# An ordered seven-product stage, a later S5 gate, and set-up work of block 0 placed anew

## The chip, the cores and the metric

One NeuronCore of one Trainium2 chip runs the kernel. The metric is the device time of one execution in microseconds (us); the median of three runs of the kernel before is 3021.39 us.

## The reference, cut to what matters

One layer over 2048 tokens of width 1024, in float32. The input is normalised, and one matrix gives twelve pieces of 512 columns and four merge gates of 1024 columns. Four branches read the pieces; each is gated by a SiLU path, projected to 1024 columns, weighted by a sigmoid gate and summed; an output matrix follows and `x` is added.

```python
h = rms_norm(x, norm_g)
proj = h @ w_in                      # 12 * 512 + 4 * 1024 columns
a_out = s5_branch(ssm_u, ...) * silu(ssm_gate)       # diagonal state space scan, then a GLU
b_out = retention_branch(ret_q, ret_k, ret_v) * silu(ret_gate)
c_out = diff_attn_branch(diff_q, diff_k, diff_v, ...) * silu(diff_gate)
m_out = memory_branch(mem_q, mem_n, ...) * silu(mem_gate)
br = einsum('bsnc,ncd->bsnd', stack(a_out, b_out, c_out, m_out), w_branch)
out = x + sum(sigmoid(merge + b_merge) * br, n) @ w_out
```

## The kernel before, in words

The tokens go in two blocks of 1024, one after the other through the same stages. Every float32 product is made of three matmuls on a high and a low part of each operand (`mm3`): ACT casts the high part (`hi`), DVE or POOL subtracts it from the value for the low part (`lo`).

**Stages of a block**, with their stretches in block 0 and block 1: retention (8 to 332 us and 1499 to 1730 us), differential attention with the S5 input at its end (to 682 and 2216 us), the seven-product stage (to 1140 and 2667 us), merge of the branches with memory attention and the S5 gate beside it (to 1399 and 2921 us), output (to 1499 and 3016 us).

**Retention** (L896 to L966) works in 32 units of four heads by eight token tiles. `Events` holds each step with a time in units: project, scale, turn (L913), score (L922), values (L930 to L940), finish, store. In block 0, events before unit 6 load, scale and turn the input tiles (`Norm`, L564 to L589), `setup_vectors` (L142) issues 15 small DMAs and one transpose, and `setup_s5` (L179) is advanced nine steps a unit from unit 6 on. For each of four groups of four S5 pairs it makes `gm` and turns it (L371), reads and turns `cm` (L388), makes `ca`, and multiplies `ca` by `bb` (L425).

**The seven-product stage** (`projections`, L1398) forms 2x2 block products with seven instead of eight multiplications. One column pair is first done plainly, four products of 24 matmuls of 128x512 (`proj_tr`). Meanwhile `x_mix` (L1368) makes the mixed inputs t2, t3, t4, t1 for four slices k. Then 21 column pairs run seven products each, 147 steps of 12 matmuls. `prepare(g + LEAD)` makes the weight of the product four steps ahead (ACT `p_h` L1304, POOL `p_l` L1305, DVE sums L1315 to L1329), `product` issues the matmuls (L1343), `collect` combines PSUM banks on DVE (L1352 to L1364) and stores. In 16 S5 scans, one for every seven steps, `s5_scan` (L998 to L1048) does two matmuls (L1002), a rotation, a scan (L1019) and another rotation on DVE, then four matmuls (L1033, L1034) that read `s_x` (L1027, L1028); `carry` is saved by L1029.

**Merge** (`Merge.run`) has 32 units of 24 matmuls: a branch product gets its gate in DVE (L1276), and POOL adds it to `merged` (L1277). Branch data come back from DRAM through four raw buffers `w_r` that weights share (`load`, L1221 to L1223). Beside the merge run the memory attention, then the S5 gate: `s5_z` reads z, `s5_zsplit` splits it (ACT L1064, DVE L1066), `s5_glu` multiplies and gates it (ACT L1088). **Output** splits `merged` (L1525, L1526), multiplies by `w_out`, and adds `x` (L1539).

**What sets the order.** Every engine takes its instructions in the order of its queue. A list scheduler of the framework fixes these orders when the kernel is built: the place in the program is a priority, and an instruction whose inputs the scheduler takes for ready may go ahead. Pools are given out again by address, so a tile waits for the last user of its space.

## Time and profile before

| what | us |
|---|---|
| median of three runs (3019.27 to 3024.44) | 3021.39 |
| the profiled execution | 3017.78 |
| its span, first to last instruction | 3016.0 |
| PE busy | 2872.6 |
| DVE busy | 1958.8 |
| ACT busy | 1336.7 |
| POOL busy | 1234.1 |

The profiled execution's time has 1.8 us around its span. PE is TensorE's matmul row, DVE VectorE, ACT ScalarE, POOL GpSimd, SP the queue that issues nearly all DMAs. PE's busy time also holds what a lower granted clock adds.

### The profile page before, as it was taken

To read this page: it belongs to the slowest core of one execution; us is meant where nothing else is said; L and a number is where in the kernel's file an instruction comes from. 1 tells how busy PE (TensorE), PEld (TensorE's weight loads), DVE (VectorE), ACT (ScalarE), POOL (GpSimd) and SP (SyncE) were. 2 spreads that over 40 slices of the span, in tenths; PEclk is the share of its full clock that TensorE was granted. 3 is DMA by queue.
4 is the path that set the end of the run, shared out by engine and by line. 5 is a ranking of instruction groups with operands and counts; after the bars stand their busy time and mean duration, and the time that the engine had idled before them with its cause. 6 is when DMAs were issued, how large, how long until landed. Compare 5 with 4: busy or idle time off the path is not lost. (4 is left out here: it accounts for less than half of the span.)

```text
span 3016.0 us, 43039 instructions
## 1 busy us (share of the span) xinstructions
PE 2872.6 (95%) x14258; PEld 2372.2 (79%) x14258; DVE 1958.8 (65%) x4622; ACT 1336.7 (44%) x3365; POOL 1234.1 (41%) x1157
## 2 busy tenths in 40 slices
PE   7888999998999999999999999999999999999999
PEld 6776777777888888777788878778878888887777
DVE  7785477766756645656543378888777666546654
ACT  4223355563343344423433357776743444444332
POOL 3443543324444443555132242332244444435660
PEclk9999999999999999999999999999999999999999
DMA  4433422223444336555521220220224444355552
GB/s 135 108 96 85 124 67 71 71 89 122 147 154 147 132 110 207 191 181 168 162 78 37 64 72 17 63 62 17 64 96 148 154 147 142 126 189 170 190 173 92
DMA packets 319645, 351.74 MB, mean 117 GB/s; under 512 B 26735, under 2 KB 238782, under 8 KB 319422
## 3 DMA queue, kind: packets, MB, share of 16 engines
q1 hardware_dynamic: 317118, 340.60, 35.9%
q0 software_dynamic: 2304, 8.39, 0.9%
q8 instruction: 112, 1.84, 0.3%
q14 instruction: 111, 0.91, 0.1%
HBM read 247.99 MB, written 100.93 MB: 116 GB/s over the span
## 5 line engine op out<-in xcount | busy, mean ns | idle before, releaser
L1305 POOL TENSOR_TENSOR p_l<-p_r,p_h 128x512 fp32r<-128x512 f32 x260 | 359.8, 1387 | 439.9 <-ACT p_h L1304 436.9
L74 PE MATMUL mm<-w5h,xh 128*128 128x512 f32 x1024 | 436.7, 426 | 5.5 <-ACT xh L588 2.7
L75 PE MATMUL mm<-w5l,xh 128*128 128x512 f32 x1024 | 406.8, 397 | 3.1 <-POOL w5l L454 3.0
L76 PE MATMUL mm<-w5h,xl 128*128 128x512 f32 x1024 | 408.9, 399 | 0.0
L138 POOL TENSOR_TENSOR rms_r<-rms_m,mhalf 128x1 f32<-128x1 f32 (+1 forms) x228 | 177.1, 778 | 498.9 <-DVE rms_m L136 428.4
L1304 ACT CAST p_h<-p_r 128x512 fp32r<-128x512 f32 x260 | 160.3, 621 | 365.7 <-DVE p_r L1318 109.4
L769 ACT ACTIVATE pr<-sc,nm 128x512 f32<-128x512 f32 (+3 forms) x320 | 200.4, 627 | 148.2 <-DVE nm L767 146.6
L76 PEld LDWEIGHTS mm<-w5h,xl 128*128 128x128 f32 x1024 | 194.8, 190 | 44.1 <-issue 0.4
L74 PEld LDWEIGHTS mm<-w5h,xh 128*128 128x128 f32 x1024 | 195.9, 191 | 36.1 <-ACT xh L588 3.1
L75 PEld LDWEIGHTS mm<-w5l,xh 128*128 128x128 f32 x1024 | 196.0, 191 | 31.8 <-POOL w5l L454 4.3
L75 PE MATMUL sc<-br_l,w1h 128*128 128x512 f32 x496 | 197.1, 397 | 7.6 <-DVE br_l L1223 7.6
L74 PE MATMUL sc<-br_h,w1h 128*128 128x512 f32 x496 | 200.3, 404 | 3.8 <-DVE mg_g L1276 3.6
L767 DVE TENSOR_REDUCE nm<-sc 128x1 f32<-128x512 f32 (+3 forms) x320 | 193.1, 604 | 9.0 <-PE sc L763 5.0
L76 PE MATMUL sc<-br_h,w1l 128*128 128x512 f32 x496 | 196.3, 396 | 0.0
L1277 POOL TENSOR_TENSOR mg<-mg,mg_g 128x512 f32<-128x512 f32 x96 | 142.0, 1483 | 88.4 <-DVE mg_g L1276 80.3
L817 PEld LDWEIGHTS o<-vt,at 128*128 128x128 f32 x1088 | 141.0, 191 | 38.3 <-ACT at L810 30.2
L817 PE MATMUL o<-vt,at 128*128 128x128 f32 x1088 | 150.9, 278 | 17.2 <-ACT at L810 17.1
L471 POOL TENSOR_TENSOR w1l<-w_r,w1h 128x512 fp32r<-128x512 f32 x86 | 119.4, 1402 | 114.2 <-ACT w1h L470 107.1
L454 POOL TENSOR_TENSOR w5l<-w_r,w5h 128x512 fp32r<-128x512 f32 x72 | 96.9, 1350 | 114.4 <-ACT w5h L453 79.6
L1343 PE MATMUL sc<-xl,p_h 128*128 128x512 f32 x336 | 131.3, 391 | 3.4 <-DVE xl L1378 3.4
L1343 PE MATMUL mm<-xh,p_h 128*128 128x512 f32 x336 | 133.7, 398 | 0.3 <-ACT p_t L1413 0.3
L1343 PE MATMUL sc<-xh,p_h 128*128 128x512 f32 x336 | 131.4, 391 | 1.0 <-ACT p_h L1304 0.5
(397 smaller groups left out, 7654.2 us busy)
## 6 DMA issues: line engine op xcount, KB each, us to landing
p_r<-in_w_in SPq DMA_DIRECT2D x88, 512.0 KB
w_r<-in_w_in SPq DMA_DIRECT2D x144, 256.0 KB
me_d<-p_t SPq DMA_DIRECT2D x128, 256.0 KB
mg_g<-me_d SPq DMA_DIRECT2D x64, 512.0 KB
s_m<-mats_d SPq DMA_DIRECT2D x32, 640.0 KB
w_r<-in_w_branch SPq DMA_DIRECT2D x64, 256.0 KB
w_r<-br SPq DMA_DIRECT2D x64, 256.0 KB
n_x<-in_x SPq DMA_DIRECT2D x16, 512.0 KB
```

The source lines that it names most:

```text
L74: PE.matmul(out, l[0], r[0], start=first, stop=False)
L75: PE.matmul(out, l[0], r[1], start=False, stop=False)
L76: PE.matmul(out, l[1], r[0], start=False, stop=last)
L138: G.tensor_tensor(r, m, mhalf[:, 0:n], op=ALU.pow)
L471: G.tensor_tensor(lo, raw, hi.bitcast(F32), op=ALU.subtract)
L767: V.tensor_reduce(nm, s[:, 0:n], axis=AX.X, op=ALU.max, negate=True)
L769: A.activation(e[:, 0:n], s[:, 0:n], AF.Exp, bias=nm, accum_out=self.zz[:, m, c:c + 1])
L817: PE.matmul(self.o[:, 0:128], self.at[c][:, q * 128:(q + 1) * 128], self.st["vts"][c][:, q, :], start=c == 0 and q == 0, stop=c * 4 + q == ...
L1277: G.tensor_tensor(dst, dst, t, op=ALU.add)
L1304: A.copy(hi, x)
L1305: G.tensor_tensor(lo, x, hi.bitcast(F32), op=ALU.subtract)
L1343: PE.matmul(o, l[:, k, :], r, start=first and k == 0 and q == 0, stop=k == 3 and q == 2, skip_group_check=True)
```

## The change

- **Ordered stage.** The whole of `projections` is put under `tc.manual_schedule` for DVE, ACT, POOL and PE: these engines keep the order of the program there. DMAs on SP are not ordered.
- **Its start.** `x_mix` yields after each cast and each subtraction and makes t1 before t4; its steps are written between the plain products, t4's behind the first three steps of the seven-product loop. The two low parts of the first column go from POOL to DVE. The S5 pool opens at step 5, and the first scan's loads move from step 1 to step 5.
- **Its end.** Branch 2's data are requested five to six steps ahead of their split; the first branch weight is read at step n - 10 and split at n - 5.
- **Set-up.** `cm` and `ca` are made ahead of `gm`'s transposes; one yield fewer a group.
- **Block 0.** Retention's values, finish and store come 0.4 units later. Input tiles have five buffers and are loaded a unit earlier; `setup_vectors` moves from 0.3 to 2.5.
- **Merge.** Branch data get four raw buffers of their own (`b_r`), gate tiles four buffers. From unit 16 on the second half's add is done by DVE. z is read at q = 7 of the loop, split from 10, multiplied from 26 (before: 0, 4, 20).
- **Output.** The residual is read two tiles ahead into three buffers; the sums have two.

```diff
+    ORDERED = {x.engine for x in (V, A, G, PE)}
...
             tt(gm[:, 1], tmp[0], tmp[1], ALU.add)
             yield
-            yield
+            cm = p.tile([16, 2, 2 * m, 64], F32, name="cm")
+            for i, nm in enumerate(("ssm_c_re", "ssm_c_im")):
+                DMA.dma_start(out=cm[:, i], in_=a[nm][0].rearrange("g h p -> h g p")[:, 2 * j0:2 * j0 + 2 * m, :])
...
+            ts(ca[:, 1], tmp[0], -1.0, ALU.mult)
             yield
             for j in range(0, m, 2):
                 pt = ps_tr()
...
-            cm = p.tile([16, 2, 2 * m, 64], F32, name="cm")
...
-            ts(ca[:, 1], tmp[0], -1.0, ALU.mult)
             yield
             yield
             for g2 in range(2):
...
-            self.x = self.p.tile([128, D], F32, name="n_x", bufs=(3, 2)[b])
+            self.x = self.p.tile([128, D], F32, name="n_x", bufs=(5, 2)[b])
...
-                events.at(i + 3.3, x.values)
-                events.at(i + 4.1, x.finish)
+                late = (0.4, 0.0)[b]
+                events.at(i + 3.3 + late, x.values)
+                events.at(i + 4.1 + late, x.finish)
                 if t % 4 == 3:
-                    events.at(i + 4.7, x.store)
+                    events.at(i + 4.7 + late, x.store)
...
             self.w0 = self.cx.enter_context(pool("w0", side="right"))
-            self.raw = self.raw_w(0)
...
+        def request(self, n, k):
+            raws = []
+            for hf in range(2):
+                if self.rp is None:
+                    raw = rawp.tile([128, 512], F32, name="w_r", bufs=4)
+                else:
+                    raw = self.rp.tile([128, 512], F32, name="b_r", bufs=4)
+                DMA.dma_start(out=raw, in_=br_d[n][self.b][k][:, hf * 512:hf * 512 + 512])
+                raws.append(raw)
+            return raws
+        def load(self, n, k, raws=None):
             hi, lo = self.pair()
+            raws = raws or self.request(n, k)
             for hf in range(2):
                 s_ = slice(hf * 512, hf * 512 + 512)
-                raw = rawp.tile([128, 512], F32, name="w_r", bufs=4)
-                DMA.dma_start(out=raw, in_=br_d[n][self.b][k][:, s_])
+                raw = raws[hf]
                 A.copy(hi[:, s_], raw)
                 V.tensor_tensor(lo[:, s_], raw, hi[:, s_].bitcast(F32), op=ALU.subtract)
...
+            self.rp = self.gx.enter_context(pool("brraw", side="right"))
...
-                t = self.gp.tile([128, TB], F32, name="mg_g", bufs=3)
+                t = self.gp.tile([128, TB], F32, name="mg_g", bufs=4)
...
                         V.scalar_tensor_tensor(t, t, 1.0, o, op0=ALU.add, op1=ALU.mult)
-                        G.tensor_tensor(dst, dst, t, op=ALU.add)
+                        (V if hf and u >= 16 else G).tensor_tensor(dst, dst, t, op=ALU.add)
...
-        def split(self, x):
+        def split(self, x, eng=G):
...
-            G.tensor_tensor(lo, x, hi.bitcast(F32), op=ALU.subtract)
+            eng.tensor_tensor(lo, x, hi.bitcast(F32), op=ALU.subtract)
...
         def split(t, d):
             A.copy(d[0][:, k, :], t)
+            yield
             V.tensor_tensor(d[1][:, k, :], t, d[0][:, k, :].bitcast(F32), op=ALU.subtract)
+            yield
...
+        yield from split(t2, xs["t2"])
+        yield from split(b12, xs["t3"])
+        yield from split(t1, xs["t1"])
         t4 = raw(x0h, x0l, 4 + k, "x_c", 2)
         V.tensor_tensor(t4, t4, xs["t2"][0][:, k, :].bitcast(F32), op=ALU.subtract)
         V.tensor_tensor(t4, t4, xs["t2"][1][:, k, :].bitcast(F32), op=ALU.subtract)
-        split(t4, xs["t4"])
-        yield
-        split(t1, xs["t1"])
-        yield
+        yield from split(t4, xs["t4"])
...
+        with pool("xs") as xsp, pool("pw") as pw, pool("pe") as pe, tc.manual_schedule(engines=ORDERED):
...
-            with pool("xm", side="right") as xm:
-                for u, x in enumerate(pairs):
-                    x.pr = (pw, first.pr)[u % 2]
-                pairs[0].load()
-                ws = [[first.split(first.raw[kh][:, :, i, :]) for kh in range(2)] for i in range(2)]
-                mixes = [x_mix(b, k, xs, xm) for k in range(4)]
-                for q, (i, hf) in enumerate(((0, 1), (1, 1), (0, 0), (1, 0))):
-                    for x in mixes:
-                        next(x)
-                    if q == 2:
-                        for g in range(LEAD):
-                            prepare(g)
-                    o = ps_mm()
-                    drain(proj_tr(o, b, hf, ws[i]))
-                    t = pe.tile([128, 512], F32, name="p_t", bufs=7)
-                    first.sink(i, hf, o, t)
-            sx = ExitStack()
-            sp = sx.enter_context(pool("s5a", side="right"))
...
+            ws = [[first.split(first.raw[kh][:, :, i, :], G if i else V) for kh in range(2)] for i in range(2)]
+            mixes = [x_mix(b, k, xs, xm) for k in range(4)]
+            def plain(i, hf):
+                o = ps_mm()
+                drain(proj_tr(o, b, hf, ws[i]))
+                t = pe.tile([128, 512], F32, name="p_t", bufs=7)
+                first.sink(i, hf, o, t)
+            def step(*ks):
+                for k in ks:
+                    next(mixes[k])
+            step(0, 1, 0)
+            plain(0, 1)
+            step(2, 1)
+            plain(1, 1)
+            step(3, 2, 3)
+            step(0, 1, 0, 2, 1, 3, 2, 3)
+            plain(0, 0)
+            step(0, 1, 0, 2, 1, 3, 2, 3)
+            for g in range(LEAD):
+                prepare(g)
+            plain(1, 0)
+            late = {0: (0, 1, 0, 1), 1: (2, 2), 2: (3, 3)}
+            sx, sp = ExitStack(), []
             side = {}
             def scan(j):
-                loaded = s5_load(b, j, sp)
+                loaded = s5_load(b, j, sp[0])
                 yield
-                yield from s5_scan(b, j, sp, *loaded)
+                yield from s5_scan(b, j, sp[0], *loaded)
             for j in range(NPAIR):
                 gen = scan(j)
-                for at in (1, 7, 8, 9, 10, 11, 13):
+                for at in (1 if j else 5, 7, 8, 9, 10, 11, 13):
                     side.setdefault(7 * j + at, []).append(gen)
             n = len(steps)
             for g, (u, s) in enumerate(steps):
+                if g == 5:
+                    mx.close()
+                    sp.append(sx.enter_context(pool("s5a", side="right")))
                 prepare(g + LEAD)
                 pairs[u].product(s)
                 pairs[u].collect(s)
+                for k in late.get(g, ()):
+                    next(mixes[k])
                 for gen in side.get(g, []):
                     next(gen)
-                if g == n - 24:
+                if g == n - 26:
                     sx.close()
                     ux.close()
                     mg.prefetch()
-                if n - 24 <= g < n - 6 and (n - g) % 6 == 0:
-                    mg.load(2, (g - n + 24) // 6)
-                if g == n - 7:
+                if g in (n - 30, n - 24, n - 17):
+                    raws = mg.request(2, (g - n + 30) // 6)
+                if g in (n - 25, n - 18, n - 11):
+                    mg.load(2, (g - n + 25) // 7, raws)
+                if g == n - 10:
+                    mg.raw = mg.raw_w(0)
+                if g == n - 5:
                     mg.first()
...
+        def residual(i):
+            if i < len(units):
+                eh, t = units[i]
+                xrs[i] = gp.tile([128, 512], F32, name="mg_x", bufs=3)
+                r0 = b * TB + t * 128
+                DMA.dma_start(out=xrs[i], in_=a["x"][0][r0:r0 + 128, eh * 512:(eh + 1) * 512])
+        for i in range(2):
+            residual(i)
...
-            xr = gp.tile([128, 512], F32, name="mg_t", bufs=5)
+            residual(i + 2)
+            xr = xrs.pop(i)
             r0 = b * TB + t * 128
-            DMA.dma_start(out=xr, in_=a["x"][0][r0:r0 + 128, eh * 512:(eh + 1) * 512])
...
-            ob = gp.tile([128, 512], F32, name="mg_t", bufs=5)
+            ob = gp.tile([128, 512], F32, name="mg_t", bufs=2)
...
-            z = s5_z(b, sp)
-            zsplit = s5_zsplit(z)
             ws = {}
-            glus = chain_of(s5_glu(b, e, mg.w1, sp, z, ws) for e in range(4))
             for q in range(128 - MEM_STEPS + 64):
                 next(merge)
-                if q == 12:
+                if q == 7:
+                    z = s5_z(b, sp)
+                    zsplit = s5_zsplit(z)
+                    glus = chain_of(s5_glu(b, e, mg.w1, sp, z, ws) for e in range(4))
+                if q == 18:
                     ws[0] = s5_wg(mg.w1, 0)
-                if 4 <= q < 20 and q % 2 == 0:
+                if 10 <= q < 26 and q % 2 == 0:
                     next(zsplit)
-                if q >= 20:
+                if q >= 26:
                     next(glus, None)
...
-                    ev.at(0.3, setup_vectors, np_)
+                    norms[3].load()
+                    ev.at(2.5, setup_vectors, np_)
                     for i in range(6):
                         x = norms[i + 2]
-                        if i < 5:
-                            ev.at(i, norms[i + 3].load)
+                        if i < 4:
+                            ev.at(i, norms[i + 4].load)
```

## Rows read from the trace of the kernel before

**Rows 1.** Page, part 1: busy us (share of the span) and instructions of each engine.
```profile
PE 2872.6 (95%) x14258; PEld 2372.2 (79%) x14258; DVE 1958.8 (65%) x4622; ACT 1336.7 (44%) x3365; POOL 1234.1 (41%) x1157
```

**Rows 2.** Waits of PE: who waited on whom: us in total, times, longest us.
```profile
PE tr L371 <- DVE gm L186: 10.5, 6, 2.7
...
PE sc L75 <- DVE br_l L1223: 7.6, 2, 3.8
PE mm L74 <- ACT g_t L1088: 6.8, 2, 4.2
PE sc L930 <- DVE rsm L922: 6.1, 4, 2.7
PE tr L585 <- DVE rms_m L136: 4.8, 1, 4.8
PE sc L1343 <- ACT p_h L1304: 4.1, 2, 3.6
PE mm L74 <- DVE mg_t L1539: 3.7, 2, 2.4
PE sc L74 <- DVE mg_g L1276: 3.6, 2, 1.8
...
PE sc L74 <- ACT br_h L1222: 3.3, 3, 1.7
```

**Rows 3.** Windows: length, busy (x count) PE PEld DVE ACT POOL, granted clock, DMA, GB/s.
```profile
682.20:737.20 55.00, 46.31 (x180) 36.82 (x179) 34.07 (x52) 19.38 (x34) 24.60 (x16) 0.88 0.34 111
2215.90:2263.90 48.00, 43.26 (x179) 34.07 (x179) 34.26 (x45) 18.84 (x34) 24.40 (x14) 0.96 0.37 126
1121.10:1140.10 19.00, 19.00 (x85) 15.76 (x84) 3.48 (x6) 5.62 (x9) 3.76 (x4) 1.00 0.28 90
737.20:1140.10 402.90, 402.90 (x1874) 337.01 (x1873) 236.77 (x420) 161.81 (x275) 180.67 (x138) 1.00 0.42 138
100.00:260.00 160.00, 140.21 (x771) 110.59 (x770) 128.71 (x393) 41.17 (x137) 71.65 (x65) 0.98 0.42 100
1140.10:1399.20 259.10, 242.61 (x1137) 198.22 (x1137) 161.19 (x268) 96.21 (x203) 143.55 (x106) 0.98 0.60 187
2667.20:2920.90 253.70, 240.55 (x1138) 197.01 (x1137) 160.16 (x268) 96.17 (x203) 143.28 (x104) 0.99 0.61 192
```

**Rows 4.** Timeline of ACT, start of the seven-product stage, block 0: start, length, line.
```profile
692.72 0.59 ACT L1413 COPY p_t<-mm 128x512 f32<-128x512 f32 x1 [9.60 <-PE mm L76]
```

**Rows 5.** Timeline of DVE, the same stretch.
```profile
694.58 1.29 DVE L1378 TENSOR_TENSOR x_t2l<-x_f,x_t2h 128x512 fp32r<-128x512 f32 x2 [9.99 <-ACT x_t2h L1377]
```

**Rows 6.** Timeline of SP's queue, first 60 us.
```profile
27.34 7.87 SPq L568 DMA_DIRECT2D n_x<-in_x  x3
```

**Rows 7.** Timeline of ACT in the merge of block 0.
```profile
1264.89 8.29 ACT L1064 ACTIVATE zh<-z_st 128x1024 fp32r<-128x1024 f32 x4 [8.46 <-DMA z_st<-z_d]
...
1324.67 0.62 ACT L1222 CAST br_h<-w_r 128x512 fp32r<-128x512 f32 x1 [7.46 <-DMA w_r<-br]
```

**Rows 8.** Groups of DVE, 740 to 1130 us: count | busy us, mean ns | idle before.
```profile
L1029 DVE COPY carry<-s_x 128x2 f32<-128x2 f32 x16 | 20.0, 1252 | 0.0
L1352 DVE TENSOR_TENSOR p_t<-sc,p_t 128x512 f32<-128x512 f32 x20 | 13.8, 692 | 15.0 <-PE sc L1343 9.6 <-issue 4.6 <-ACT p_t L1350 0.3
L1019 DVE TENSOR_TENSOR_SCAN s_y<-rho,carry,s_w 128x128 f32<-128x128 f32 x32 | 13.8, 472 | 0.6
...
L1329 DVE TENSOR_TENSOR p_r<-p_r 128x512 f32<-128x512 f32 x19 | 13.1, 692 | 21.3 <-POOL p_l L1305 21.3
...
L1008 DVE TENSOR_TENSOR s_q<-s_y,s_m 64x256 f32<-64x256 f32 x16 | 10.9, 680 | 0.5
...
L1028 DVE TENSOR_TENSOR s_x<-s_q,s_q 128x256 f32<-128x256 f32 x16 | 6.7, 420 | 0.0
...
L1027 DVE COPY s_x<-carry 128x2 f32<-128x2 f32 x15 | 2.4, 161 | 0.0
```

**Rows 9.** Page, part 5: a group of POOL, its columns as in rows 8.
```profile
L1305 POOL TENSOR_TENSOR p_l<-p_r,p_h 128x512 fp32r<-128x512 f32 x260 | 359.8, 1387 | 439.9 <-ACT p_h L1304 436.9
```

More of the change, by code (lines that the diff above doesn't have):

```diff
@@ L365, in setup_s5 @@
             yield
-            yield
-            yield
-            for j in range(0, m, 2):
-                pt = ps_tr()
-                for q in range(4):
-                    PE.transpose(pt[:, q * 128:(q + 1) * 128],
-                                 gm[:, q % 2, j + q // 2].rearrange("p s h -> p (s h)"), ident)
-                ev = p.tile([128, 2, 256], F32, name="ev", bufs=1)
-                for q in range(2):
-                    A.copy(ev[:, q, :].rearrange("p (g i s) -> p i g s", g=2, i=2),
-                           pt[:, q * 256:(q + 1) * 256].rearrange("p (i g s) -> p i g s", g=2, i=2))
-                DMA.dma_start(out=mats_d[:, j0 + j:j0 + j + 2, 0:256], in_=ev)
-                yield
             cm = p.tile([16, 2, 2 * m, 64], F32, name="cm")
@@ L408, in setup_s5 @@
             ts(ca[:, 1], tmp[0], -1.0, ALU.mult)
+            yield
+            for j in range(0, m, 2):
+                pt = ps_tr()
+                for q in range(4):
+                    PE.transpose(pt[:, q * 128:(q + 1) * 128],
+                                 gm[:, q % 2, j + q // 2].rearrange("p s h -> p (s h)"), ident)
+                ev = p.tile([128, 2, 256], F32, name="ev", bufs=1)
+                for q in range(2):
+                    A.copy(ev[:, q, :].rearrange("p (g i s) -> p i g s", g=2, i=2),
+                           pt[:, q * 256:(q + 1) * 256].rearrange("p (i g s) -> p i g s", g=2, i=2))
+                DMA.dma_start(out=mats_d[:, j0 + j:j0 + j + 2, 0:256], in_=ev)
+                yield
             yield
@@ L1377, in split @@
             A.copy(d[0][:, k, :], t)
+            yield
             V.tensor_tensor(d[1][:, k, :], t, d[0][:, k, :].bitcast(F32), op=ALU.subtract)
+            yield
         t1 = raw(x0h, x0l, k, "x_a", 4)
@@ L1403, in projections @@
               "22": (x1h[:, 4:8, :], x1l[:, 4:8, :]), "t1": (x1h[:, 0:4, :], x1l[:, 0:4, :])}
-        with pool("xs") as xsp, pool("pw") as pw, pool("pe") as pe:
+        with pool("xs") as xsp, pool("pw") as pw, pool("pe") as pe, tc.manual_schedule(engines=ORDERED):
             ux = ExitStack()
@@ L1467, in projections @@
-            sx = ExitStack()
-            sp = sx.enter_context(pool("s5a", side="right"))
+            mx = ExitStack()
+            xm = mx.enter_context(pool("xm", side="right"))
+            for u, x in enumerate(pairs):
+                x.pr = (pw, first.pr)[u % 2]
+            pairs[0].load()
+            ws = [[first.split(first.raw[kh][:, :, i, :], G if i else V) for kh in range(2)] for i in range(2)]
[5 more added lines that the diff above has]
+                first.sink(i, hf, o, t)
```

10 lines of the change are left out of this document (2 added, 8 removed).

## The prediction

> **What bounds the kernel now.** I read the page's first part, then PE's waits, then windows by stage, then timelines where a wait was long. PE is busy 2872.6 of 3016.0 us [rows 1]; the rest, 143 us, is what an edit of order can win, and whatever the lower granted clock adds to the busy time. The waits show that this idle time lies in many places of a few us each, and that one line often waits twice, once in each block: br_l 7.6 in 2, g_t 6.8 in 2, mg_g 3.6 in 2 [rows 2]. What recurs in both blocks comes from the order of the queues and not from chance. The windows tell where PE is full: in the steady part of the seven-product stage it is busy 402.9 of 402.9 us at clock 1.00 [rows 3]. There is nothing to win there, only something to lose.
>
> **The change part by part.** A measurement tells 0.2% (6 us) from no change. The sum is made against the profiled execution, 3017.8 us.
>
> *Start of the ordered stage.* Seven products, 84 matmuls, take 19.0 us where nothing is in the way [rows 3], 0.226 us each, 2.71 us for a product. The four plain products and the first seven steps have 96 + 84 = 180 matmuls, so 40.7 us. They took 55.0 in block 0 and 48.0 in block 1 [rows 3]: 14.3 and 7.3 us lost, the first at a mean clock of 0.88. The cause is visible: ACT sat 9.60 us in front of a copy of the first plain product, with the t2 casts behind it [rows 4], and DVE waited 9.99 us for those casts [rows 5]; later PE waited for p_h [rows 2]. In the new order two t2 casts stand ahead of that copy, and the other two behind one copy each, while DVE has other mixes to make. I walk DVE's queue through: two low parts at 0.69, 24 sums and 4 t2 low parts, then 8 low parts of t3 and t1 and three weight sums, some 41 instructions at about 0.6 us each, 25 us from the moment the first p_h is cast, against 21.7 us of plain products plus the first step. The work fits within about 2 us. What now waits behind DVE's two low parts are all mixes, for some 5 us, and PE does not need a mix before the second step. t4 needs 20 more instructions, 13 us, and is due five steps in, 13.6 us. I leave 2 us lost in block 0 and 1 in block 1: **12 and 6 us won** (bounds 5 to 14 and 2 to 7).
> The first scan's loads have two products, 5.4 us, instead of six. No row shows their landing. 640 KB at the stage's 138 GB/s [rows 3] are 4.6 us; at half of that 4 us would be missing in each block. Nearest to the first: **1 us lost** (0 to 9).
>
> *Steady part.* The order on PE is the same. On DVE each scan step now stands behind its step's collect. **0** (bounds: the slower rival, below, and nothing to gain).
> *End of the stage.* Requests go out five or more products, 13 us, ahead of their splits, and first() still has five products for a cast and a subtraction: hidden by PE's own queue; without that cover 2 us.
>
> *Set-up.* PE waits 10.5 us for gm at L371 [rows 2]; all its idle time between 100 and 260 us is 160.0 - 140.2 = 19.8 [rows 3]. The ca sums, seven DVE or POOL instructions, now lie between gm and its transposes; the transposes in turn lie between ca and L425. The two cm loads and eight small transposes of a group go ahead of gm's four by a few instructions on SP and PE: under 1 us a group, hidden by the loads' early issue. But DVE is busy 128.7 of these 160 us; were all idle time gone, it would be busy 92% of what is left, and late in turn. **8** of 19.8 (0 to 19.8).
> *Values later.* PE waits 6.1 us for rsm [rows 2]. 0.4 units are some 4 us more, longer than the longest wait of 2.7. Banks and tiles are held as much longer; three banks carry it. **4.5** (0 to 6.1).
> *Tiles and vectors.* SP stood 7.87 us issuing three input tiles [rows 6], blocked on buffers, behind 15 small DMAs; PE waited 4.8 us for a norm's rms_m [rows 2]. Five buffers let the loads go, and the 15 DMAs pass behind them. The same POOL powers meet other work two units later. **3.5** (0 to 4.8).
>
> *Merge.* Named waits are br_l 7.6, g_t 6.8, mg_g 3.6 [rows 2], 18.0 us over both blocks. Clock means of 0.98 in 259.1 us and 0.99 in 253.7 [rows 3] are worth 5.2 and 2.5 us more at most. br_l was late behind z's casts, which hold ACT for 8.29 us [rows 7], and z now comes after those loads in the program; g_t was late behind a cast on ACT that waited 7.46 us for branch data read into the shared buffers [rows 7], and these data get their own. The added waits: z's four loads, issued later, have 19 merge steps until the multiplication instead of 20; and the gate's last store comes six steps nearer to its reading, with some 10 us left. 16 adds a block at about 0.69 go to DVE, 11 us, which is busy 161 of 259 us there [rows 3]. **16** of 25.7 (5 to 25.7).
> *Into the merge and output.* br_h 3.3 and mg_t 3.7 [rows 2]: their engines wait as much for other things in the queue as for data. **1 and 2** (0 to 7 together). Two buffers for the sums leave 24 matmuls, 5.4 us, and one more for a store to go out: hidden; without it a us a tile.
>
> Sum: 12 + 6 - 1 + 0 + 8 + 4.5 + 3.5 + 16 + 1 + 2 = 52 us. 3017.8 - 52 = 2965.8. The profiled execution lies 3.6 under the median of the runs, so the median should be **2969**.
>
> **The rivals.**
> *Idle time that moves.* Set-up, merge and output keep three quarters of their waits in new places, because DVE is full (set-up) or ACT still takes things in an unlucky order. The ordered stage's 17 us stay, and a quarter of the other 35 is 9: 26 won, 2995 us. For it: DVE's 92%; against it: most merge waits have one cause each.
> *The edits outside the ordered stage do nothing.* There the place in the program is only a priority, and the queues may come out as before. Then 17 us: 3004. For it: the mixes of the stage that the change rewrites ran far from their place in the program [rows 4, 5]; against it: a late load or a missing buffer is no matter of priority.
> *The scan arrives late, and the kernel is slower.* Place: the four matmuls that read s_x, 16 times a block. From the end of a pair's second product the ordered DVE does L1352 0.69, one 256-wide sum 0.42, two scans 0.94, two 0.42 and one 0.68 for the rotation, L1329 0.69, L1027 0.16, L1028 0.42 [rows 8]: 4.84 us. PE has two products until it needs s_x, 5.43 us. The slack is 0.6 us. A 128x2 copy takes 0.16 as L1027 and 1.25 as L1029 [rows 8], which runs beside a p_l on POOL: DVE loses 1.09 us there. Two p_l of 1.39 [rows 9] fall into two products. If both stopped this chain fully, s_x would be 4.84 + 2.78 - 5.43 = 2.2 us late, and 32 such waits cost 70 us: 2969 + 70 = **3039**. From 52 / 32 = 1.6 us the gain is gone, from 1.8 it measures slower. Against it: the sums and scans of the same chain, run beside p_l's before too, lose at most 0.26 each (L1008 0.68 to 0.42) [rows 8], and in the new order p_l of one step follows a cast that waits for L1329, so POOL is free during most of the chain.
> The Trainium skill (SBUF — State Buffer, section "SBUF: two separate sides") says that DVE and GpSimd share a port pair under an exclusive lock, by which the later of two contending instructions waits out the other. By that rule the rival's full stop is possible, and L1027, now right ahead of L1028, could be stopped like L1029. L1029's row agrees with it; the sums' rows show much less than a full stop.
>
> **How the numbers follow.** The forecast, 35 to 75 us won: 0.55. More than that: 0.05. Idle time that moves: 0.12; nothing outside the ordered stage: 0.08. Scan 1.2 to 1.8 us late or the gains given back otherwise, within 0.2%: 0.07. Slower: 0.13, most of it the scan. Faster is 0.55 + 0.05 + 0.12 + 0.08 = 0.80. All upper bounds together (14.3 + 7.3 + 19.8 + 6.1 + 4.8 + 25.7 + 7) are 85 us, 2936; the range starts at 2938 and goes to 3010, behind 2995 and 3004, and leaves out same and slower, 0.20. The forecast's own range is 2946 to 2986.
>
> **What would show it.** Right: the two windows from the first plain product to the eighth step near 43 us at a clock near 1; no wait for p_h or p_l there; no wait for br_l and g_t in the merge; L371's wait under 3 us. Wrong: waits of L1034 for s_x, or of L1002 for the first scan's loads; DVE over 90% in the set-up with new waits for gm or rsm; new waits on ACT behind z's casts. The forecast fails if PE's idle time is the same but elsewhere.

## The result, and the profile after

The changed kernel takes 3002.2 us (median of 4 runs, 2998.8 to 3009.8), the kernel before 3020.6 beside it: ratio 0.994, 95% interval 0.9919 to 0.9962. It is faster by 18 us where 52 were forecast. The profiled execution took 3003.0 us, its span is 3001.2.

The first part of the page, and PE's waits (us in total, times, longest us), answer to [rows 1, 2]:

```profile
PE 2867.9 (96%) x14258; PEld 2368.2 (79%) x14258; DVE 1944.2 (65%) x4658; ACT 1312.6 (44%) x3365; POOL 1175.2 (39%) x1121
...
PE sc L75 <- ACT br_h L1233: 9.0, 4, 3.4
PE sc L920 <- ACT rqkT L916: 8.4, 5, 3.3
...
PE tr L401 <- DVE gm L187: 6.9, 5, 2.1
PE sc L76 <- DVE br_l L1234: 4.9, 2, 2.5
PE sc L1355 <- DVE p_t L1364: 4.9, 2, 2.4
PE sc L1355 <- DVE p_t L1367: 4.6, 2, 2.3
PE mm L75 <- DVE rg L623: 4.5, 5, 1.6
```

PE is busy 4.7 us less, and stands 10 us less. The waits for g_t (6.8), rsm (6.1), p_h (4.1) and rms_m (4.8) of [rows 2] are gone; gm's is 6.9 instead of 10.5. But five lines are new or have grown: rqkT (ACT's copy of the turned q and k) 8.4 and rg (DVE's product for retention) 4.5, two collects of the seven-product stage (L1364 and L1367, DVE's sums that read a PSUM bank and so free it) 9.5, and br_h 9.0 where 3.3 stood. Windows show in which stages that lies: the set-up's part of [rows 3], then for block 0 the four plain products, the first seven steps and the rest of the stage, then the first two for block 1, then both merges.

```profile
100.00:260.00 160.00, 139.39 (x743) 108.64 (x742) 128.32 (x384) 38.30 (x132) 68.30 (x63) 0.95 0.43 102
684.70:706.40 21.70, 21.70 (x97) 17.98 (x96) 21.49 (x35) 9.74 (x17) 0.82 (x2) 1.00 0.35 109
706.40:736.30 29.90, 22.36 (x86) 16.56 (x84) 25.41 (x28) 9.86 (x18) 15.44 (x10) 0.94 0.33 98
736.30:1140.50 404.20, 403.91 (x1873) 336.66 (x1872) 223.60 (x423) 152.01 (x275) 185.28 (x141) 1.00 0.43 140
2204.90:2226.60 21.70, 21.70 (x97) 18.00 (x96) 18.15 (x28) 9.53 (x17) 1.52 (x1) 1.00 0.26 86
2226.60:2254.80 28.20, 22.07 (x86) 16.61 (x85) 23.67 (x27) 9.86 (x18) 13.45 (x9) 0.94 0.34 106
1140.50:1388.10 247.60, 238.25 (x1137) 196.39 (x1136) 161.59 (x283) 96.12 (x202) 125.03 (x91) 0.99 0.61 196
2659.00:2908.80 249.80, 239.83 (x1138) 197.54 (x1137) 162.41 (x283) 95.86 (x202) 124.33 (x91) 0.98 0.61 194
```

The plain products are now full in both blocks: 21.7 us at clock 1.00, where 27.0 and 22.2 stood. The seven steps are not: 29.9 and 28.2 against 19.0 for 84 free matmuls, and against 28.4 and 26.2 before. The merges went from 259.1 and 253.7 [rows 3] to 247.6 and 249.8. The set-up has the idle time it had, 160.0 - 139.4 = 20.6 us against 19.8 [rows 3].

By stage, in us: to the first transposes of kn, the end of block 0's retention (called first kn from here on), +3.4; plain products -5.6 over both blocks; seven steps +3.4; rest of the stage +1.9; merges -15; output -1; the attention stages changed by about 1 us or less each. Only the merge came out as forecast, as a sum.

The queue behind the seven steps' waits is DVE's (timeline: start us, length us, line, idle before it):

```profile
709.69 0.69 DVE L1385 TENSOR_TENSOR x_c<-xh,xl 128x512 f32<-128x512 f32 x1
710.41 0.69 DVE L1405 TENSOR_TENSOR x_c<-x_c,x_t2h 128x512 f32<-128x512 f32 x1
711.13 1.65 DVE L1406 TENSOR_TENSOR x_c<-x_c,x_t2l 128x512 f32<-128x512 f32 x1
712.71 1.78 DVE L1385 TENSOR_TENSOR x_c<-xh,xl 128x512 f32<-128x512 f32 x1
714.52 1.66 DVE L1405 TENSOR_TENSOR x_c<-x_c,x_t2h 128x512 f32<-128x512 f32 x1
716.22 1.66 DVE L1406 TENSOR_TENSOR x_c<-x_c,x_t2l 128x512 f32<-128x512 f32 x1
717.81 1.45 DVE L1391 TENSOR_TENSOR x_t4l<-x_c,x_t4h 128x512 fp32r<-128x512 f32 x2
719.17 0.69 DVE L1364 TENSOR_TENSOR p_t<-sc,p_t 128x512 f32<-128x512 f32 x1
710.50 1.73 POOL L1317 TENSOR_TENSOR p_l<-p_r,p_h 128x512 fp32r<-128x512 f32 x1 [2.08 <-ACT p_h L1316]
```

The collect L1364, which frees the bank that the fourth product adds into, could have run when the second product ended, before 715; it runs at 719.17, behind eight instructions for t4, which is not due before 725. PE waits 2.43 us for it. And the same sum takes 0.69 us in one place and 1.65 to 1.78 in another, where a p_l runs on POOL (the first such p_l is the last row).

### The profile page after: what moved, and what is told of

Its sections match the earlier page's. It is cut to its first block, busy times and chain, and to the rows that moved or that the text cites. A ratio compares the mean times of both kernels' runs of the same rounds, so it can differ in the third digit from the quotient of the medians.

```text
span 3001.2 us, 42941 instructions
## 1 busy us (share of the span) xinstructions
PE 2867.9 (96%) x14258; PEld 2368.2 (79%) x14258; DVE 1944.2 (65%) x4658; ACT 1312.6 (44%) x3365; POOL 1175.2 (39%) x1121
## 5 line engine op out<-in xcount | busy, mean ns | idle before, releaser
L1317 POOL TENSOR_TENSOR p_l<-p_r,p_h 128x512 fp32r<-128x512 f32 x256 | 348.5, 1368 | 497.0 <-ACT p_h L1316 493.4
L1289 POOL TENSOR_TENSOR mg<-mg,mg_g 128x512 f32<-128x512 f32 x64 | 95.9, 1502 | 116.0 <-DVE mg_g L1288 88.0
L1438 ACT ACTIVATE p_t<-p_t,vec 128x512 f32<-128x512 f32 x96 | 69.5, 724 | 157.1 <-DVE p_t L1367 75.4
```

Of the source, the lines that this page charges most:

```text
L1317: eng.tensor_tensor(lo, x, hi.bitcast(F32), op=ALU.subtract)
```

## The experiments

Each run changes one thing in the changed kernel unless its edit says otherwise, and is timed against the kernel before on its own chip; ratios are to that.

### The set-up, values and tiles of block 0

Edits: the three parts of the change put back as in the kernel before, one at a time, then all.

```diff
e1: gm's transposes ahead of the ca sums again
e2: -late = (0.4, 0.0)[b]
    +late = (0.0, 0.0)[b]
e3: n_x bufs 3, loads at i of norms[i + 3], setup_vectors at 0.3
e4: all three
```

> Undone: only the set-up's transposes go back ahead of the ca sums. First kn comes at 365.3 us in the changed kernel, at 361.9 in the kernel before. Theory 1 (idle time moves: DVE is the set-up's bound, so a wait for gm that goes comes back for another DVE result): the wait of the gm transposes grows from 6.9 to about 10 us, the new waits of 4.5 for rg and 3.4 for ca shrink by as much, first kn at 363 to 367, total within 3 us. Theory 2 (the new order itself costs, since the ca sums delay other DVE work): first kn at 361 or less, total 4 us or more below. The prediction's term would make it 8 us slower.

> Undone: only block 0's later values and finish (0.4 units back to 0). Theory 1 (idle time moves): the wait for rsm comes back at some 6 us, while waits for on and rqkT (2.4 and 8.4) shrink; first kn at 363 to 368, total within 3 us. Theory 2 (this part does harm: it holds banks and tiles longer, which makes the rqkT waits): rqkT waits under 4 us, first kn at 361 or less. The prediction's term would make it 4.5 us slower, first kn at 370.

> Undone: only the input tiles (three buffers, loads one step later) and the small vectors' place. Theory 1 (idle time moves): the norm's wait for rms_m comes back, 4 to 5 us, and the rqkT waits of 8.4 us between 68 and 99 us go; first kn at 362 to 367. Theory 2 (the placing does harm, as the vectors' POOL and DVE work now falls where the first tiles' q and k are made): rqkT waits under 3 us, first kn at 360 or less, total 5 us or more below. The prediction's term would make it 3.5 us slower.

> Undone: all three block-0 edits; the ordered stage, the merge and the output stay changed. First kn should come where the kernel before has it, 361.9 us (360.5 to 363.5), as nothing ahead of it differs from that kernel. Theory 1 (the three edits together cost 3.4 us because the idle time only moved): total 2999 to 3000, 3 us below the changed kernel. The prediction's terms (8 + 4.5 + 3.5) would make it 16 us slower.

Measured: 2999.5 us, ratio 0.9929 (0.9910 to 0.9947); 2995.0, 0.9919 (0.9902 to 0.9936); 3001.6, 0.9940 (0.9923 to 0.9956); 2995.2, 0.9918 (0.9903 to 0.9932). First kn came at 363.0, 360.4, 365.2 and 357.0 us. None of the three was worth what was forecast, and the values had the wrong sign: putting them back wins. The gm wait at the transposes, which the set-up's edit was made for, is 6.7 us in e4 as well, where the old order stands, so its fall from 10.5 to 6.9 is not shown to be that edit's. With the values late, PE's waits between 40 and 110 us are the first pair of lines, with them back (e2) the second:

```profile
PE sc L920 <- ACT rqkT L916: 8.2, 4, 3.3
PE mm L75 <- DVE rg L623: 3.0, 3, 1.6
```

```profile
PE sc L930 <- DVE rsm L922: 4.2, 3, 2.8
PE mm L75 <- DVE rms_m L137: 2.8, 1, 2.8
```

That is 11.2 us of waits for the later values and 7.0 for the early ones. The likely reading is that the wait for rsm had covered the copy rqkT, and that without it the next score waits.

How much of such differences is chance was asked by running the changed kernel once more:

> The changed kernel once more, on the chip of these runs, as a measure of how far a stage repeats: first kn at 365.3 within 2 us, from the first plain product to the merge 455.8 and 454.1 within 1 us, merge 247.6 and 249.8 within 2 us, total 2999 to 3005.

It took 3007.3 us, ratio 0.9945 (0.9928 to 0.9962). The ordered stage takes 455.8 and 454.1 us again, to 0.1 us; the first stretch does not repeat: first kn at 370.8. Over this run, the first profile and the ten runs below that leave block 0's set-up and retention alone it comes at 365.1 to 370.8, mean 367.1. The order of the queues up to there is the same in these twelve, so their spread of nearly 6 us lies in the execution. The two runs with all three parts put back (e4, and e13 below) have 357.0 and 355.7. The windows up to that point, of the changed kernel twice, then of e4:

```profile
0.00:365.30 365.30, 316.98 (x1616) 253.75 (x1617) 251.18 (x785) 118.97 (x354) 148.66 (x157) 0.97 0.40 110
```

```profile
0.00:370.80 370.80, 326.22 (x1617) 259.51 (x1618) 251.17 (x785) 119.19 (x354) 148.71 (x157) 0.95 0.40 108
```

```profile
0.00:357.00 357.00, 315.71 (x1616) 253.38 (x1617) 248.48 (x785) 122.18 (x354) 148.38 (x157) 0.98 0.42 113
```

The three parts together cost about 11 us by first kn (367.1 - 356.4), 7 to 11 by the ratios of whole runs (0.9918 against 0.994 and 0.9945; 0.9873 for e13 against 0.9908 for e11). PE's idle time is 41.3 in e4 against 48.3 and 44.6 in the changed kernel, whose matmuls also take longer, at a lower clock: 1.3 us in the one run and 10.5 in the other. The kernel before has the same text there as e4 and came to 361.9 in its profile, with queues in another order in this stretch, although the two programs differ only far behind it. So differences of 5 to 6 us there come without a cause in the edit, and the 11 is rough. e3 lies within the spread of the twelve, e1 2 us and e2 5 us below it, one profile each: the late values are the part that costs most.

Why the later values cost was tried once. ACT's scaling of on, which waits for POOL's rms_r, stands in ACT's queue right ahead of a later tile's rqkT copy, and comes with the values. e14 takes it off ACT:

```diff
-head_scale(self.on, self.r)
+G.tensor_tensor(o3, o3, bc(self.r, 2, 128), op=ALU.mult)   # block 0's retention
```

> In block 0's retention the scaling of on by rms_r goes from ACT to POOL, which makes rms_r; values and finish stay as late as in the changed kernel. Theory (later values cost because the finish that moves with them puts ACT's scaling, which waits for POOL's rms_r, right ahead of a later tile's rqkT copy): rqkT waits fall from 8.4 to under 3 us between 60 and 105 us, the rsm wait stays away, first kn at 358 to 362. Rival (the copy rqkT is late for its buffers or for DVE's chain): rqkT waits stay at 6 us or more, first kn at 363 to 368. Second rival (POOL's scaling holds DVE off, or rqk and rms_r on POOL come later): the waits move to rqk or gm, first kn at 364 or more.

3006.5 us, 0.9945 (0.9928 to 0.9962). The rqkT waits fell to 5.0, not under 3 (the changed kernel's second run has 6.0 between 40 and 110 us, without any edit), and first kn came at 370.0: other DVE results were late instead. That copy's place is a part of the cause at most; the rest stays open.

### The start of the ordered stage

e7 gives the low parts of the first pair to DVE, to ask why its sums are slow:

```diff
-pairs[u].prepare(s)
+pairs[u].prepare(s, G if u else V)      # engine of p_l
```

> The seven p_l of the first pair are made by DVE instead of POOL. Theory 1 (DVE's sums of two SBUF operands take 1.65 to 1.79 us instead of 0.69 because POOL's p_l runs beside them): the t4 sums take 0.69 each, the 20 t4 instructions 14 us instead of 19 although seven p_l of 0.69 join them, and the waits for the collects fall from 2.4 to under 1 us; the two waits for p_l (1.45 and 0.79) become shorter, as 0.69 takes the place of 1.39 or more: 2 to 4 us a block won. Rival (the sums are long for a reason of their own, as their operands): they stay at 1.6 to 1.8, DVE has 4.8 us more to do and the waits for the collects grow by as much: 3 to 5 us a block lost.

3005.3 us, 0.9937 (0.9919 to 0.9955). The same six sums in its timeline:

```profile
716.22 0.69 DVE L1385 TENSOR_TENSOR x_c<-xh,xl 128x512 f32<-128x512 f32 x1
716.94 0.69 DVE L1405 TENSOR_TENSOR x_c<-x_c,x_t2h 128x512 f32<-128x512 f32 x1
717.66 0.69 DVE L1406 TENSOR_TENSOR x_c<-x_c,x_t2l 128x512 f32<-128x512 f32 x1
718.27 0.68 DVE L1385 TENSOR_TENSOR x_c<-xh,xl 128x512 f32<-128x512 f32 x1
718.99 0.69 DVE L1405 TENSOR_TENSOR x_c<-x_c,x_t2h 128x512 f32<-128x512 f32 x1
719.72 0.69 DVE L1406 TENSOR_TENSOR x_c<-x_c,x_t2l 128x512 f32<-128x512 f32 x1
```

All at 0.69: the 1 us that four of them lost was POOL's p_l beside them. Little time was won: the stage to the merge took 453.9 and 453.6 us, where runs that leave the stage alone have 455.8 or 454.2 and 454.1 or 452.5 (see the last section). Six p_l joined DVE's queue ahead of the collect, whose wait grew from 2.4 to 3.5 in block 0. So the queue's length counts, whoever fills it.

e6 puts the first six sums into the 4.6 us that DVE stands idle ahead of the stage:

```diff
+ws = [[first.high(x) for x in raws[0]]]          # p_h alone
+next(mixes[0])                                   # six sums, cast of t2
+ws[0] = [first.low(x, *hl, V) ...]               # then p_l
```

> The first tile's six sums go ahead of the two low parts of the weights in DVE's queue, into the 4.6 and 5.8 us that DVE stands waiting for the cast p_h. In the changed kernel the stretch from the first plain product to the first t4 product takes 40.9 and 39.1 us (156 matmuls, 35.3 at 0.226), and t4 and the next product wait 2.9 us more. Theory 1 (DVE's queue at the start is too long, and collects that free banks stand behind its mixes): everything on DVE comes 4 us earlier, the waits of 2.43 for the collect L1364 and 2.30 for L1367 go, and those for p_l too or stay: the stretch takes 37 to 38.5 and 36 to 37 us, 4 to 6 us a block in all. Rival (POOL's low parts and ACT's casts set the pace, DVE's queue does not): the waits stay within 0.5 us of what they were, total within 2 us. Second rival: the first plain product waits for its own p_l, as much as the sums take: 4 us lost ahead of it.

3003.6 us, 0.9936 (0.9921 to 0.9951). The stage to the merge went from 455.8 and 454.1 to 452.5 twice. In block 1 that is not the edit's: four runs that leave the stage alone have 452.5 there too. In block 0 their lower value is 454.2, so 1.7 us can be the edit's, a p_l's wait of 1.45 that is gone. The first collect is as late as before (2.40 and 2.44): DVE lost its head start to two sums of 1.78 beside a p_l of POOL and to 1.3 us of waiting for an ACT cast. The theory's size is missed: an earlier start does not help the order of what stands in front.

e11 takes four sums out of that place:

```diff
+t2 = raw(x1h, x1l, 4 + k, "x_f", 4)              # kept
 t4 = raw(x0h, x0l, 4 + k, "x_b", 4)
-V.tensor_tensor(t4, t4, xs["t2"][0]...)
-V.tensor_tensor(t4, t4, xs["t2"][1]...)
+V.tensor_tensor(t4, t4, t2, op=ALU.subtract)
```

> t4 is made from the t2 that is kept in one tile (one subtraction) and not from its two parts (two): four sums of the start's DVE queue are gone in each block, all of them among the t4 mixes that stand ahead of the collects. Theory 1 (the waits of 2.43 and 2.30 us for the collects are the length of that queue): two sums of 1.65 go ahead of the first collect and four ahead of the second; the waits fall to under 1 us and under 0.5 us, t4's own 0.6 goes, and the half clock of 3 us behind them with it: from the first plain product to the merge 455.8 and 454.1 become 450 to 452 in both blocks, 6 us below the changed kernel in all. Rival (the collects stand behind something else, as the casts x_t4h on ACT): waits stay above 2 us, within 2 us of the changed kernel.

2995.4 us, 0.9908 (0.9887 to 0.9930). Its seven steps in block 0 and block 1, as windows:

```profile
707.50:732.60 25.10, 20.57 (x84) 15.49 (x85) 22.40 (x24) 8.62 (x17) 14.09 (x9) 1.00 0.30 95
...
2226.80:2249.90 23.10, 19.93 (x86) 15.56 (x85) 20.31 (x23) 8.71 (x16) 12.67 (x8) 1.00 0.33 108
```

These are 25.1 and 23.1 instead of 29.9 and 28.2; the two collect waits are 1.05 and 1.34, and the clock stays at 1.00 where 0.94 stood. The stage to the merge takes 451.6 and 449.0, 9.3 us less over both blocks, where the theory gave 6 with waits under 1 and 0.5. The waits shrank less than it said; more than it said came from the slow stretch of the clock behind them, which is gone in both blocks, worth some 1.6 us in each (last section). Against the runs whose slow stretch falls behind the first wait the gain is about 6.

e5 drops the order by hand:

```diff
-..., pool("pe") as pe, tc.manual_schedule(engines=ORDERED):
+..., pool("pe") as pe:
```

> The order by hand of the ordered stage is dropped, the program's text stays: the planner sets the queues there again. Theory 1 (most of what the stage's start won comes from the mixes' new sequence and the placing, and the planner would serve collects before mixes): from the first plain product to the merge 452 to 456 us as now, total within 3 us. Rival (the order by hand is what holds t2's casts ahead of the copies of the plain products): the start takes 55 us and more again in block 0, total 5 to 10 us above the changed kernel. Second rival (the order by hand costs in the steady part, where the fm distance grew by 0.24 us in the silu units): 3 us a block less.

3002.0 us, 0.9927 (0.9904 to 0.9951). The plain products are full there too, and the rest of the stage has the old length:

```profile
688.10:709.90 21.80, 21.80 (x98) 18.06 (x97) 21.80 (x34) 9.62 (x16) 2.09 (x2) 1.00 0.35 108
...
737.10:1140.00 402.90, 402.90 (x1874) 337.01 (x1873) 236.63 (x420) 161.79 (x275) 181.26 (x139) 1.00 0.43 141
```

The seven steps have other waits, 3.95 for a p_l and, in block 1, 8.3 for L1364 again; in all the stage takes 451.9 and 454.3. So the order by hand is worth nothing here: the plain products are full without it, by what else the change does at the stage's start (which part of that was not tried), and it costs 1.3 us a block in the rest, all of it in the third to sixth of the 21 pairs.

### The merge

e10 undoes the later gate, e9 the branch data's own buffers, e16 the sums on DVE, e17 the fourth gate buffer.

```diff
e10: z at q == 1, zsplit from 4, gate from 20      (was 7, 10, 26)
e9:  -self.rp = self.gx.enter_context(pool("brraw", side="right"))
e16: -(V if hf and u >= 16 else G).tensor_tensor(dst, dst, t, ...)
     +G.tensor_tensor(dst, dst, t, ...)
e17: "mg_g", bufs=3
```

> Undone: only the later place of z's loads, casts and multiplication (six merge steps earlier again, as in the kernel before). Theory 1 (the place in the program does next to nothing here, since the queues outside the ordered stage take z's casts whenever the data are there: ACT has them in front of the same four br_h casts in both): merge within 1 us of 247.6 and 249.8, the waits for br_h and br_l unchanged. The prediction's reason (z behind those loads frees br_l) would make the merge 4 us a block longer.

> The branch data of the merge go through the shared raw buffers again, as in the kernel before; the later gate, four mg_g and the sums on DVE stay. Theory (the wait for g_t, 6.8 us over both blocks before, went because the branch casts no longer hold ACT for shared buffers): g_t waits of 5 to 7 us are back, merge 6 to 9 us longer over both blocks. Rival (the wait for g_t went for another reason, the later gate or the sums on DVE): no g_t wait, merge within 2 us of 247.6 and 249.8.

> Undone: only the merge's 16 sums a block that go to DVE; POOL makes them all again. Theory (these sums are what took the wait for g_t, 6.8 us over both blocks before, away, by freeing POOL where w1l and the sums met): waits for g_t or w1l of 4 us or more come back, merge 4 to 7 us longer over both blocks than 247.6 and 249.8. Rival (they are beside the path): merge within 2 us of these.

> Undone: only the fourth gate buffer mg_g of the merge. Theory (the fourth buffer is what shortened the waits behind mg_g from 3.6 to 2.5 us and took the wait for g_t away): these waits come back, merge 3 to 7 us longer over both blocks. Rival (a gate's data are there in time with three): merge within 2 us.

Times and ratios: e10 3001.7, 0.9932 (0.9915 to 0.9950); e9 3006.1, 0.9947 (0.9929 to 0.9965); e16 3003.1, 0.9943 (0.9926 to 0.9960); e17 3002.8, 0.9943 (0.9928 to 0.9958). The merges took 246.2 and 247.6 us in e10, 251.6 and 253.1 in e9, 247.9 and 248.3 in e16, 247.1 and 250.5 in e17. How far such a time repeats is told by the twelve runs that leave the merge alone (the changed kernel twice, e1 to e7, e11, e13, e14): both merges together take 494.7 to 501.2 us, mean 497.4. Only e9 lies clear of that, at 504.7: the buffers carry 7.3 us of the 15. e10, at 493.8, lies 0.9 below the lowest: the later gate is worth nothing, and that it costs is not clear. The other two lie inside. No single one brings the wait for g_t back, so which edits took it away stays open, and with it half of the 15. What the buffers do is seen in the first 16 us of block 0's merge, of the changed kernel and of e9, and in ACT's waits in that merge of e9:

```profile
1140.00:1156.00 16.00, 14.83 (x74) 12.12 (x74) 7.91 (x16) 8.35 (x18) 7.07 (x6) 1.00 0.95 337
1138.80:1154.80 16.00, 14.01 (x55) 11.49 (x55) 5.38 (x10) 5.24 (x9) 5.53 (x5) 0.79 0.84 279
ACT w1h L470 <- DMA w_r<-in_w_branch: 24.9, 15, 4.3
```

In e9 PE stands 2.0 us for br_h there instead of 1.2, the granted clock falls, and 3.9 of the 4.0 us that this merge is longer are lost by its third unit; block 1 loses as much there. Behind that, PE's named waits are no longer than in the changed kernel. ACT's cast of the branch weights waits 24.9 us for data, 15 times; with buffers of their own for the branch data most of that line's waiting is for PE. So the gain of the buffers lies at the merge's start, not at g_t; that the late weights make it is likely, not shown.

br_h and br_l still wait. ACT in the merge of the changed kernel, to be read against [rows 7]:

```profile
1266.20 2.18 ACT L1065 ACTIVATE zh<-z_st 128x1024 fp32r<-128x1024 f32 x1 [6.43 <-DMA z_st<-z_d]
1268.13 0.67 ACT L470 CAST w1h<-w_r 128x512 fp32r<-128x512 f32 x1
1268.67 6.06 ACT L1065 ACTIVATE zh<-z_st 128x1024 fp32r<-128x1024 f32 x3
1274.49 2.22 ACT L1233 CAST br_h<-b_r 128x512 fp32r<-128x512 f32 x4
```

The program has the four br_h casts ahead of z's; the planner has them behind. e8 takes them to DVE, e12 keeps ACT's queue in the program's order:

```diff
e8:  -A.copy(hi[:, s_], raw)
     +(V.tensor_copy if n == 3 and k > 1 else A.copy)(hi[:, s_], raw)
e12: -with pool("s5b") as sp:
     +with pool("s5b") as sp, tc.manual_schedule(engines={A.engine}):
```

> The casts br_h of the last two branch tiles of the third quarter of the merge (n = 3, k = 2 and 3) go from ACT to DVE, so that they no longer stand behind z's casts. Theory 1 (br_h is late because ACT holds two or three zh casts of 2.05 us in front of it): PE's waits at that place, 3.4 for br_h and 2.4 for br_l in each block, fall to under 1.5 us together, and with them the half clock behind it; the stretch from the merge's first matmul to the first z matmul goes from 146.7 and 148.8 to 140 to 143 us, total 8 to 15 us below the changed kernel. Rival 1 (br_h is late because the tile it writes is read until 1.4 us before): waits of 2.5 to 4 us stay. Rival 2 (the wait moves): z's low parts on DVE come later and the first z matmuls wait instead, total within 3 us.

> ACT's queue from the end of the memory stage to the end of the S5 gate is kept in the order of the program, nothing else changes: the four late br_h casts now stand ahead of z's four. Theory 1 (br_h and br_l are late because of the order that the planner gives ACT: the tile is free at 1268.0 to 1268.7 and the first cast starts at 1274.5): the waits of 3.4 and 2.4 us in each block fall to under 1 us and the half clock behind them goes: merge 8 to 14 us shorter over both blocks. Rival 1 (the tile is free too late in any order): waits of 2 to 4 us stay. Rival 2 (the order of the program is worse elsewhere: w1h behind z's casts, g_t behind the branch casts): the first waits go and as much comes back at w1h or g_t, total within 3 us.

e8: 3002.5 us, 0.9933 (0.9918 to 0.9948); PE waits 4.2 and 3.7 for br_h, because the planner puts eleven zl ahead of it on DVE, 5.06 us in one row. A third rival that was not foreseen: the same order on another engine. e12: 3003.4, 0.9941 (0.9919 to 0.9964); the waits for br_h and br_l at that place are gone, and others come in: 4.3 for mg_g in block 0, 2.8 for w1l and 2.0 for zl in block 1. DVE shows why in block 0:

```profile
1277.24 9.49 DVE L1067 SCALAR_TENSOR_TENSOR zl<-z_st,zh 128x128 fp32r<-128x128 f32 x16
1286.65 0.68 DVE L1288 SCALAR_TENSOR_TENSOR mg_g<-mg_g,sc 128x512 f32<-128x512 f32 x1
```

Sixteen zl in a row hold the gate sum that frees PE's bank. The merges are 250.7 and 245.5, together 1.2 us less than in the changed kernel, which is within the spread: ACT's order was the cause of that wait, and curing it moves the wait.

### What beats both

e13 puts the three block-0 parts back and keeps t4 short (e4 with e11).

> The changed kernel with the three block-0 edits undone and t4 made from the kept t2. If the two effects add, as they lie in different stages: first kn at 357 us as with the three edits undone (8.3 below the changed kernel), the ordered stage 9.3 us shorter over both blocks as with the short t4: 2984 to 2987 us, ratio to the kernel before 0.988 to 0.990. Rival (the planner sets the set-up's order anew with every edit, and a gain there does not carry over): first kn at 361 to 366, total 2990 to 2994.

2984.7 us, ratio 0.9873 (0.9857 to 0.9889): 38 us faster than the kernel before and 22.6 faster than the changed kernel on the same chip (3007.3). The two effects add: first kn at 355.7, the stage to the merge 451.5 and 449.0.

## Why the prediction was wrong, step by step

*What bounds the kernel.* Right: the time is in many small waits of PE, and the steady part had nothing to give (402.9 became 404.2).

*Start of the ordered stage, 12 and 6 won.* Wrong; this step and that of the set-up, values and tiles make up the miss. The whole stage to the merge won 2.4 us in block 0 and lost 2.0 in block 1, where 17 were forecast in all. Its first half held: the plain products lost 5.3 and 0.4 us and lose nothing now. The sentence that failed is "t4 needs 20 more instructions, 13 us, and is due five steps in, 13.6 us". It asked when t4 is due and not what stands behind t4 on DVE: two collects that free banks. And it took about 0.65 for each instruction, where four of the first six sums took 1.65 to 1.78 beside POOL's p_l, so that t4's mixes took 19.1 us from first to last (709.69 to 728.79). A row of the kernel before, in this very stretch and beside p_l's, had shown it:

```profile
722.45 1.75 DVE L1329 TENSOR_TENSOR p_r<-p_r 128x512 f32<-128x512 f32 x1 [4.85 <-POOL p_l L1305]
```

3.4 and -1.9 were won on the two windows of [rows 3] that 12 and 6 were forecast for; e11 shows that the queue ahead of the collects makes those waits, e7 that p_l makes the sums long. The first scan's loads, put at 1 us lost, made PE wait nowhere.

*Steady part and scan.* The slower rival did not come: no wait for s_x, and PE idle 0.29 us in the 404.2. The new order put nothing of the chain beside a p_l; even the copy of carry, 1.25 us before [rows 8], is at 0.17 between 740 and 1130 us:

```profile
L1030 DVE COPY carry<-s_x 128x2 f32<-128x2 f32 x16 | 2.7, 169 | 0.5
```

Each scan step behind its collect was harmless as forecast; the order by hand costs 1.3 us, where 0 was put.

*Set-up 8, values 4.5, tiles and vectors 3.5.* The failing step is to have priced each wait by what it was, as if the next result were then there. These three terms, 16 us won, came out as 7 to 11 us lost. The text named the danger ("late in turn") and took 8 of 19.8 all the same. For the values it said that 0.4 units exceed the longest wait, and of what else moves with them it named banks and tiles only, not the finish and its queue on ACT and POOL. The wait for rsm did go, and rqkT and rg came in its place, 11.2 us for 7.0; why is open beyond what e14 shows.

*Merge 16, into it 1.* The sum was right (15) by luck, its parts were not. br_l was to come from the later gate, which is worth nothing (e10): "z now comes after those loads in the program" was taken for the queue's order, and outside the ordered stage it is none. br_l's wait fell only from 7.6 to 4.9, and br_h's grew from 3.3 to 9.0. g_t's wait went, yet not for the buffers alone; the buffers gave their 7.3 us at the merge's start, and no run shows where the other half came from.

*Output 2.* About 1, in size within the noise of these stages.

*The rivals.* "Idle time that moves" is the case that came in set-up, values and tiles, and beyond what it allowed, as they ended below nothing; but its 17 us for the ordered stage did not hold either, so its sum of 2995 missed by 7. "The edits outside the ordered stage do nothing" has the number, 3004, for the wrong reasons. The range held the time.

*Where a rule was used.* The prediction used the shared lock of the Trainium skill (SBUF — State Buffer, section "SBUF: two separate sides") for the scan, where it did no harm, and not for its own first term, where sums of the same size run beside p_l. The trace agrees with it there: 0.69 alone, 1.65 to 1.78 beside, and 0.69 again once POOL made no p_l (e7). A slow sum starts while a p_l runs and ends some 0.55 us after it (711.13 + 1.65 = 712.78, against 710.50 + 1.73 = 712.23): it loses about what is left of that p_l, 1.0 to 1.1 us, and not a whole one.

## What to carry to other kernels

When a step of DVE is given a due time, list what stands behind it in the queue, above all the reads that free a PSUM bank, and price its instructions beside POOL's, not alone. Where an engine is 80% busy over a stretch, a wait that is removed has a successor: name the next late result and subtract it, and check what else an event drags with it. Outside a part ordered by hand, the place in the program is not the place in the queue; a gain forecast there has to exceed the spread that comes without it, here 5 to 6 us in the first 365. And a gain in a stretch with waits has to exceed what the clock behind the waits gives and takes by itself, here 1.6 us a block.

## What the runs showed of the hardware that was not expected

A wait of PE can cost more than itself, and it is not settled which wait does. In the changed kernel the clock is granted at full level behind the first collect's wait of 2.43, and mostly at the half level (1.2 instead of 2.4 GHz) behind the second's of 2.30. In e10, whose program is the same in the ordered stage, it is the other way round. Windows of 3.6 us behind the first and the second wait, of the changed kernel and then of e10:

```profile
720.00:723.60 3.60, 3.60 (x16) 2.97 (x17) 2.85 (x4) 0.62 (x1) 0.40 (x1) 1.00 0.00 0
731.50:735.10 3.60, 3.23 (x8) 2.55 (x9) 2.21 (x4) 1.80 (x4) 1.10 (x1) 0.55 0.92 238
724.20:727.80 3.60, 3.58 (x9) 2.83 (x10) 2.85 (x4) 0.62 (x1) 0.42 (x1) 0.53 0.00 0
735.80:739.40 3.60, 3.31 (x14) 2.74 (x15) 2.38 (x5) 1.88 (x4) 1.18 (x1) 1.00 0.88 240
```

The 3.6 us hold 16 matmuls at full level and 8 or 9 in the slow stretch, some 1.6 us less of work. Behind the first wait that stretch gives DVE time for its queue, as its sums keep their 0.69 us there but for one: the second wait is then 1.80 to 1.88, and the seven steps take 28.3 and 26.6 us instead of 29.9 and 28.2. Thirteen runs have this stage as in the changed kernel; in three of them in block 0, and in five in block 1, the slow stretch came first. So a program that repeats to 0.1 us in one more run can still differ by 1.6 us a block in the next.

And two executions of the same program, on two chips, differ by 9 us in PE's busy time up to first kn (317.0 and 326.2, clocks 0.97 and 0.95), in queues of the same order: a gain of a few us in a stretch where PE stands often is not read from one profile.
